# A transformer layer's first stage: from a simulated schedule to a written order of half-tile slots

## The chip, the cores and the metric

The kernel runs on one core of a Trainium2 chip. The metric is the device time of one execution in microseconds (us); the time of a kernel is the median of several runs. Engines are called PE (TensorE: products), PEld (its weight loads), DVE (VectorE), ACT (ScalarE), POOL (GpSimd) and SP (SyncE, which here issues DMAs). "Clock" is the share of the TensorE clock that was granted.

## What is computed

One layer of a diffusion transformer with two mixers side by side, for 2048 positions of width 1024, with 256 context positions that supply keys, values and a start state:

```python
mod = (silu(c) @ w_mod + b_mod)                    # sh1, sc1, g1, sh2, sc2, g2
h  = rmsnorm(x, norm1_g) * (1 + sc1) + sh1         # the same for ctx: hc
rq, rk, rv, rg, aq, ak, av = split(h @ w_in)       # hc gives rk, rv, ak, av only
ret = bidir_retention(rope(rq), rope(rk), rv)      # 4 heads of 128, chunks of 128
ret = groupnorm(ret) * gn_g * silu(rg)
att = attention(rope(rmsnorm(aq)), rope(rmsnorm(ak)), av)   # 8 heads of 64, 2 kv heads
x = x + g1 * (concat(ret, att) @ w_out)
x = x + g2 * (relu(h2 @ w_ff1) ** 2 @ w_ff2)       # h2: rmsnorm and modulate again
return rmsnorm(x, final_norm_g)
```

Everything is float32 in and out. Products that matter are made of float16 halves: an operand is split into a high and a low half, and three products (high by high, high by low, low by high) are added in PSUM.

## The kernel before, in words

The kernel has a first stage, an attention stage beside which retention and the output product run, and the feed-forward stage. The diff touches the first stage and a few lines of attention.

**First stage.** There are 18 tiles of 128 positions (2 of context, 16 of the sequence). First the modulation (class `Modulation`): 8.4 MB of `w_mod` come in 16 pairs of loads through four buffers of the tag `wst`, and small products with the activated `c` (L322) sum them into PSUM; `shift_and_scale` and `balance_h` make from them the factors `a1`, `s1` and the power of two `bk`. Then `h` is made per tile: load x, sum of squares (L405), root on POOL (L79, L80), scaling (L407), transposes (L432), modulation (L434, L435) and the split into halves (L70, L71). All 18 `h` tiles stay in SBUF.

Then the input product goes over six blocks of columns in the order `C_RV, C_RK, C_AKV, C_AQ, C_RG, C_RQ`; within a block it goes over the tiles (18 for RV, RK and AKV, 16 for the rest). A row, one tile by one block, is 24 products on PE (L504 to L506; AKV is half as wide). The weights of a block (class `Weights`) are loaded, their absolute sums are taken on ACT (L462), a scale is made from them and from `bk` (`scales`), and they are split on ACT and DVE (L488, L489). Behind a row, `post` evacuates PSUM on ACT and does what the column needs: rotary embedding on DVE and POOL (L535 to L542), norms, transposes on PE (L590, L621, L652), and stores to DRAM by SP.

Beside the rows, "extra" work is woven in by credits (`ROOM`, `share`): the later modulation rows (`later_rows`: load `wmr`, add on DVE at L356, product with ones at L368) and the largest absolute values of the other weights (`weight_maxima`: load `wm`, reduce on DVE at L711 or sum on ACT at L714). `value_parts`, `decay_tables` and `ff_scales` stand in the list `spare`, one step per row. `first_maximum` makes the row maxima of the first attention group in RG, 18 pieces, each a product into one PSUM bank and a reduce on DVE (L165, L178).

The program text of this stage does not fix the order on the engines: the framework orders its instructions by a simulated timeline (`schedule_with_timeline_sim=True`). DMAs are issued by SP; the tables for the rotary embedding, the biases and the gate stores are issued by ACT.

**Attention.** Its order is written out: `on(k, phase, fn)` puts a function into step k, and the steps are run in order under `tc.manual_schedule()`. There are 32 groups (a tile of queries and one of two key heads) of 18 steps each. Group n has its maxima ("piece" and "maximum") in steps 18n to 18n + 17, and its scores (L202, L203), exponentials (L208) and value products (L235, L236) from step 18n + 22 on. Group 0's maxima come from the first stage, so steps start near 18. Retention's forward states (L1098 to L1114) run beside groups 0 and 1.

Of the kernel before, what the change touches and what calls it, by code (L numbers as in the profile page):

```python
# [11 lines left out]
F32 = mybir.dt.float32  # L12
# [24 lines left out]
PSHIFT = 8  # L37

# [16 lines left out]
def layer_kernel(ctx: ExitStack, tc: tile.TileContext, a: dict, out: bass.AP):  # L55
# [85 lines left out]
    class Group:  # L141
# [15 lines left out]
        def minima(self, pool):  # L157
            self.nm = pool.tile([P, 2, 2, 5], F32, name="nm", tag="nm")
# [101 lines left out]
    with ExitStack() as st:  # L260
        xp = st.enter_context(tc.tile_pool(name="xp", bufs=4, reuse_waits="tile"))
        tp = st.enter_context(tc.tile_pool(name="tp", bufs=2, reuse_waits="tile"))
        hp = st.enter_context(tc.tile_pool(name="hp", bufs=1, reuse_waits="tile"))
        wp = st.enter_context(tc.tile_pool(name="wp", bufs=6, reuse_waits="tile"))
        sg = st.enter_context(tc.tile_pool(name="sg", bufs=3, reuse_waits="tile"))
# [9 lines left out]
        nc.sync.dma_start(cc, a["cc"])  # L275
        nc.scalar.activation(cc, cc, AF.Silu)
        cst = one.tile([P, KT, 2, 16], F32, name="cst")
        nc.vector.tensor_copy(cst, bc(cc.unsqueeze(3), [P, KT, 2, 16]))
        ones = one.tile([P, 32], F32, name="ones")
        nc.vector.memset(ones, 1.0)  # L280
        n1 = one.tile([P, KT], F32, name="n1")
        n2 = one.tile([P, KT], F32, name="n2")

# [8 lines left out]
        class Modulation:  # L292
# [4 lines left out]
            def __init__(self, q, b):  # L297
                self.q, self.w = q, {}
                self.b = b[:, q % 2 * self.W : (q % 2 + 1) * self.W]

            def load(self, k):
                if k == 0:
                    nc.gpsimd.memset(self.b[64:], 0.0)
                    for i in range(2):
                        c = i * D + self.q * self.W
                        src = a["b_mod"][0, c : c + self.W]
                        nc.scalar.dma_start(self.b[32 * i : 32 * i + 32], src.partition_broadcast(32))
                self.w[k] = sg.tile([P, 2, 2, self.W], F32, name="wst", tag="wst", bufs=4)
                for r in range(2):
                    rows = a["w_mod"][0, (k + r) * P : (k + r + 1) * P, : 2 * D]  # L310
                    src = rows.rearrange("p (i n) -> p i n", i=2)[:, :, self.q * self.W : (self.q + 1) * self.W]
                    nc.sync.dma_start(self.w[k][:, r], src)

            def product(self, k):
                if k == 0:
                    self.ps = psM.tile([P, 512], F32, name="mps", tag="mps")
# [7 lines left out]
            def end(self):  # L324
                nc.vector.tensor_tensor(self.b, self.ps[:, : self.W], self.b, op=ALU.add)

            def shift_and_scale(self):
                f = slice(2 * self.q, 2 * self.q + 2)
                scale = sm.tile([P, 2, 2], F32, name="sc", tag="sc")
                ps = columns(self.b, 2)  # L330
                for i, to in enumerate((s1[:, :, f].rearrange("p c j -> p j c"), scale)):
                    nc.vector.tensor_reduce(to, ps[:, :, i::2].rearrange("p j e c -> p j c e"), axis=AX.X, op=ALU.add)
# [4 lines left out]
        def later_rows(j, use):  # L337
# [4 lines left out]
            def load(i, k):  # L342
                w = x[i, k] = sg.tile([P, 2, 512], F32, name="wmr", tag="wmr", bufs=2)
# [3 lines left out]
            def add(i, k):  # L347
                w = x.pop((i, k))
                if k == 0:
                    x["acc"] = one.tile([P, 512], F32, name="macc", tag="mb")  # L350
# [6 lines left out]
                if (i, k) != (1, KT - 2):  # L357
                    load(*((i, k + 2) if k + 2 < KT else (1, 0)))

            def sums(i):  # L360
                if i == 0:
                    x["b"] = op.tile([P, 512], F32, name="mrow", tag="xs")
                    x["ps"] = psM.tile([P, 512], F32, name="mps", tag="mps")
                b, ps = x["b"], x["ps"]
                q = slice(32 * i, 32 * i + 32)
                src = a["b_mod"][0, (j + i) * 512 : (j + i + 1) * 512]
                nc.scalar.dma_start(b[q], src.partition_broadcast(32))
                mm(ps[q], ones, x["acc"], start=True, stop=True)  # L368
                if i == 1:
                    nc.vector.tensor_tensor(b[:64], ps[:64], b[:64], op=ALU.add)  # L370
                    use(b)

            steps = [lambda: load(0, 0)]
            for i in range(2):
                steps += [lambda i=i, k=k: add(i, k) for k in range(0, KT, 2)] + [lambda i=i: sums(i)]
            return steps

        def store_gate(r, b):
            for j in range(2):
                row = b[32 * j : 32 * j + 1, :]  # L380
                nc.scalar.dma_start(gate_d[r][j * 512 : (j + 1) * 512].unsqueeze(0), row)

        def shift2(b):
            ps = columns(b[:64], 4)
            nc.vector.tensor_copy(s2.rearrange("p (i j) -> p j i", i=2), ps[:, :, :, 0])

        def scale2(b):
            ps = columns(b[:64], 4)
            a, n = (x.rearrange("p (i j) -> p j i", i=2) for x in (a2, n2))
            nc.vector.scalar_tensor_tensor(a, ps[:, :, :, 0], 1.0, n, op0=ALU.add, op1=ALU.mult)  # L390

        def mod_steps():
            steps = later_rows(4, lambda b: store_gate(0, b)) + later_rows(6, shift2)
            return steps + later_rows(8, scale2) + later_rows(10, lambda b: store_gate(1, b))

        TILES = [("c", i) for i in range(NC)] + [("l", i) for i in range(NT)]

        def load_x(kind, i):

            x = xp.tile([P, D], F32, name=f"x_{kind}{i}", tag="x", bufs=4)  # L400
            src = a["ctx"] if kind == "c" else a["x"]
            nc.sync.dma_start(x, src[0, i * P : (i + 1) * P, :])
            ss = sm.tile([P, 1], F32, name="ss", tag="ss", bufs=2)
            junk = tp.tile([P, D], BF16, name="junk", tag="junk", bufs=1)
            nc.scalar.activation(junk, x, AF.Square, accum_out=ss)  # L405
            r = rsqrt(sm, ss, 1, 1.0 / D, "x")
            nc.vector.tensor_scalar_mul(x, x, r)  # L407
            return x

        bk = one.tile([P, KT], F32, name="bk")  # L410

        def balance_h():


            m = sm.tile([P, 2, KT], F32, name="hb", tag="hbm", bufs=1)
            for i, v in enumerate((a1, s1)):
                src = v.rearrange("p c k -> p k c")
                nc.vector.tensor_reduce(m[:, i], src, axis=AX.X, op=ALU.max, apply_absolute_value=True)
            nc.vector.scalar_tensor_tensor(bk, m[:, 0], 32.0, m[:, 1], op0=ALU.mult, op1=ALU.add)
            binade(bk)  # L420
            nc.vector.reciprocal(m[:, 0], bk)
            r = bc(m[:, 0].unsqueeze(1), [P, 2, KT])
            for v in (a1, s1):
                nc.vector.scalar_tensor_tensor(v, v, 4096.0, r, op0=ALU.mult, op1=ALU.mult)

        def part_h(kind, x, h, k, n):

            c = 1 if kind == "c" else 0
            f = slice(k, k + n)
            ps = psT.tile([P, 4, P], F32, name="psx", tag="psx")[:, :n]  # L430
            for j in range(n):
                nc.tensor.transpose(ps[:, j], x[:, (k + j) * P : (k + j + 1) * P], ident)  # L432
            t = tp.tile([P, 4, P], F32, name="t", tag="t")[:, :n]
# [1389 lines left out]
```

## Time and profile before

| | |
|---|---|
| median of 3 runs | 2941.21 us (2940.58 to 2946.13) |
| the profiled execution: its time | 2945.99 us |
| its span, first to last instruction | 2944.2 us |
| mean granted clock | 0.98 |
| first and last input product (pso) of the first stage | start at 65.7 and 663.5 us |
| first scores of attention | 674.1 us |

The span is some 1.8 us shorter than the device time of the same execution. In rows of busy time by stretch the columns are the stretch, its length, the busy us of PE, PEld, DVE, ACT and POOL with the number of instructions, the granted clock, the mean busy share of the 16 DMA engines, and the GB/s that they moved. In rows of groups, what follows the bar is the busy time and the mean duration in ns, then the idle time of the engine just before, with what ended it.

### The profile page before, as it was taken

The numbers are of one execution on the slowest core, as the hardware profiler recorded it, in microseconds if no ns is written. First come the engines' busy times: TensorE is split into PE (matmuls) and PEld (weight loads), VectorE is DVE, ScalarE is ACT, GpSimd is POOL, SyncE is SP. The second block draws the span as 40 slices with busy tenths as digits, with TensorE's granted clock in tenths as the row PEclk, the third lists the DMA queues.
The fourth block names the chain that finished last, engine by engine and source line by source line (L and its number), as shares of the span: only waits on it lengthen the run. The fifth ranks groups of instructions, "written<-read, shape, count | busy, mean of one in ns | idle before, by whom it ended". The sixth has DMA issues, their size and how long they took to land. (4 is left out here: it accounts for less than half of the span.)

```text
span 2944.2 us, 45374 instructions
## 1 busy us (share of the span) xinstructions
PE 2749.6 (93%) x17152; PEld 1460.0 (50%) x17152; DVE 2097.5 (71%) x3305; ACT 1429.7 (49%) x2418; POOL 1524.6 (52%) x1288
## 2 busy tenths in 40 slices
PE   5999998897799999999999899999999899999998
PEld 1544743345566665556666444444444344444443
DVE  4635665658987777777776477778777777777776
ACT  2552463135777777777777333333332333333332
POOL 1423672225865677886566556664443444444332
PEclk6999999999999999999999999999999999999999
DMA  9476457536412123332211723331114511111111
GB/s 298 141 228 208 149 162 225 164 89 211 126 48 67 56 64 113 95 103 81 87 50 51 273 91 101 104 104 63 49 51 154 174 59 47 56 49 51 58 43 58
DMA packets 252250, 323.89 MB, mean 110 GB/s; under 512 B 105463, under 2 KB 161015, under 8 KB 250238
## 3 DMA queue, kind: packets, MB, share of 16 engines
q1 hardware_dynamic: 241750, 313.49, 33.0%
q10 hardware_dynamic: 10280, 7.48, 0.9%
q8 instruction: 135, 2.21, 0.3%
q14 instruction: 85, 0.70, 0.1%
HBM read 249.45 MB, written 71.46 MB: 109 GB/s over the span
## 5 line engine op out<-in xcount | busy, mean ns | idle before, releaser
L178 DVE TENSOR_REDUCE nm<-mp 128x1 f32<-128x512 f32 (+1 forms) x576 | 390.7, 684 | 155.9 <-PE mp L165 127.5
L219 POOL TENSOR_TENSOR plo<-p,phi 128x1024 f16<-128x1024 f32 x160 | 353.3, 2209 | 172.6 <-ACT phi L212 134.5
L208 ACT ACTIVATE p<-st 128x512 f32<-128x512 f32 x576 | 338.5, 597 | 190.8 <-PE st L203 119.4
L1597 PE MATMUL pd<-w2hi,uhi 128*128 128x512 f16 x1024 | 388.0, 379 | 13.7 <-DVE acc L1600 13.6
L1598 PE MATMUL pd<-w2lo,uhi 128*128 128x512 f16 x1024 | 388.0, 379 | 0.6 <-DVE w2lo L71 0.6
L1599 PE MATMUL pd<-w2hi,ulo 128*128 128x512 f16 x1024 | 388.1, 379 | 0.0
L1600 DVE SCALAR_TENSOR_TENSOR acc<-pd,sc,acc 128x512 f32<-128x512 f32 x512 | 366.3, 738 | 5.6 <-PE pd L1599 5.6
L1537 PE MATMUL pu<-hf,w1f 128*128 128x512 f16 x896 | 340.8, 380 | 2.5 <-DVE q L1560 2.0
L1538 PE MATMUL pu<-hf,w1f 128*128 128x512 f16 x896 | 340.9, 380 | 0.0
L1539 PE MATMUL pu<-hf,w1f 128*128 128x512 f16 x896 | 340.7, 380 | 0.0
L212 ACT ACTIVATE phi<-p 128x1024 f16<-128x1024 f32 x288 | 303.9, 1055 | 0.0
L506 PE MATMUL pso<-whi,h 128*128 128x512 f16 (+1 forms) x816 | 298.1, 366 | 4.0 <-DVE h L71 3.9
L504 PE MATMUL pso<-whi,h 128*128 128x512 f16 (+1 forms) x816 | 297.3, 365 | 2.2 <-ACT h L70 2.2
L505 PE MATMUL pso<-wlo,h 128*128 128x512 f16 (+1 forms) x816 | 298.3, 366 | 0.2 <-DVE wlo L489 0.2
L235 PE MATMUL o<-wv,plo 128*128 128x65 f16 x2304 | 236.1, 194 | 23.9 <-POOL plo L219 16.7
L221 DVE TENSOR_TENSOR plo<-p,phi 128x512 f16<-128x512 f32 x256 | 240.7, 941 | 18.5 <-ACT phi L212 15.9
L236 PE MATMUL o<-wv,phi 128*128 128x129 f16 x2304 | 243.9, 221 | 0.0
L235 PEld LDWEIGHTS <-plo 128*128 128x128 f16 x2304 | 206.8, 98 | 58.7 <-POOL plo L219 25.9
L202 PE MATMUL st<-qr,ks 128*128 128x512 f16 x576 | 219.5, 381 | 15.0 <-ACT p L208 14.9
L165 PE MATMUL mp<-ks,qr 128*128 128x512 f16 x512 | 196.8, 384 | 38.3 <-DVE nm L178 38.2
L203 PE MATMUL st<-qr,ks 128*128 128x512 f16 x576 | 219.9, 382 | 0.1
L1549 POOL TENSOR_TENSOR r<-r 128x512 f32<-128x512 f32 x64 | 66.4, 1041 | 295.6 <-ACT r L1548 295.6
(338 smaller groups left out, 5407.2 us busy)
## 6 DMA issues: line engine op xcount, KB each, us to landing
wm<-in_w_ff SPq DMA_DIRECT2D x64, 512.0 KB, 5.1
w1r<-in_w_ff SPq DMA_DIRECT2D x64, 512.0 KB, 4.2
ws<-in_w_ff SPq DMA_DIRECT2D x124, 256.0 KB, 3.3
wmr<-in_w_mod SPq DMA_DIRECT2D x32, 512.0 KB, 4.9
hf<-hp SPq DMA_DIRECT2D x56, 256.0 KB, 3.1
hf<-hf SPq DMA_DIRECT2D x14, 1024.0 KB, 6.3
wst<-in_w_in SPq DMA_DIRECT2D x20, 512.0 KB, 5.4
orv<-rv SPq DMA_DIRECT2D x35, 256.0 KB, 3.3
```

The source lines that it names most:

```text
L178: nc.vector.tensor_reduce(dst, src, axis=AX.X, op=ALU.max, negate=True)
L208: nc.scalar.activation(self.p[kt // 2][:, kt % 2], self.s.pop(kt), AF.Exp, scale=HD**-0.5)
L212: nc.scalar.activation(hi, self.p[j], AF.Copy)
L219: nc.gpsimd.tensor_tensor(lo, p, hi, op=ALU.subtract)
L235: mm(o[:, : HD + 1], lo[:, i, c], v[:, : HD + 1], start=False, stop=False)
L1537: mm(pu[i], whi, hi, start=k == 0, stop=False)
L1538: mm(pu[i], whi, lo, start=False, stop=False)
L1539: mm(pu[i], wlo, hi, start=False, stop=k == 3)
L1597: mm(ps, uh, wh, start=f == 0, stop=False)
L1598: mm(ps, uh, wl, start=False, stop=False)
L1599: mm(ps, ul, wh, start=False, stop=f == NF - 1)
L1600: nc.vector.scalar_tensor_tensor(acc[:, c], ps, sc2, acc[:, c], op0=ALU.mult, op1=ALU.add)
```

## The change

The first stage gets a written order. Every row is two half-tile slots q (2s and 2s + 1 for row s); `at(q, step, fn)` puts a function into a slot, and the steps of a slot are run in the order "dma", "mm", "turn", "copy", "work", "mix", "extra", "store" under `tc.manual_schedule()`. In detail:

- A class `Row` replaces `post`, `rope` and `head_norm`: each part of what follows a row has a slot of its own, up to nine after the row's last product.
- `Modulation.load` puts the weights into the buffers of `h` (tags h2 to h17), which are not in use yet: all 16 pairs of loads are issued at once, with x tiles 0 to 3 and the first block of `w_in` between them. The biases come whole. `balance_h` becomes part of `shift_and_scale`, per quarter.
- In the start, the sums of the first `w_in` block and the first halves of three `h` tiles are made beside the modulation; the second halves and the splits follow it.
- Later rows and maxima have fixed slots: in RK and RG one later-rows load and one reduce of maxima per tile; the |w| sums on ACT four before RK, then one a tile in AKV and AQ, two in RG. `value_parts` is in AQ, `decay_tables` and `ff_scales` in RQ.
- `first_maxima` makes the maxima of three attention groups (`EARLY = 3`): group 0 in RG, groups 1 and 2 in RQ, in two PSUM banks; attention leaves out these pieces, so steps 18 to 53 have none. Groups 1 and 2 load their queries again in attention.
- PSUM: `psM` has two banks of the tag `mp` and one `mps` (one before); `psO` has 3 banks instead of 5. `tp` has 4 buffers instead of 2, `sg` 2 instead of 3 by default.
- All DMAs of the stage are issued by SP. The sum of the identity in `tables` is on POOL instead of DVE.

The diff, cut to its core:

```diff
+EARLY = 3
...
-        psM = st.enter_context(tc.tile_pool(name="psM", bufs=1, space=PSUM, reuse_waits="tile"))
+        psM = st.enter_context(tc.tile_pool(name="psM", bufs=2, space=PSUM, reuse_waits="tile"))
...
-        psO = st.enter_context(tc.tile_pool(name="psO", bufs=5, space=PSUM, reuse_waits="tile"))
+        psO = st.enter_context(tc.tile_pool(name="psO", bufs=3, space=PSUM, reuse_waits="tile"))
+        st.enter_context(tc.manual_schedule())
+        slots, base = [], {}
+        for n, col in enumerate(ORDER):
+            base[col] = 2 * len(slots)
+            slots += [(n, m) for m, t in enumerate(TILES) if t[0] == "l" or col not in (C_RQ, C_RG, C_AQ)]
+        base["end"] = 2 * len(slots)
+        STEPS = ("dma", "mm", "turn", "copy", "work", "mix", "extra", "store")
+        plan = {}
+        def at(q, step, fn, *args):
+            plan.setdefault((q, step), []).append((fn, args))
...
             def load(self, k):
-                self.w[k] = sg.tile([P, 2, 2, self.W], F32, name="wst", tag="wst", bufs=4)
+                n = 2 + self.q * 4 + k // 2
+                self.w[k] = hp.tile([P, 2, 2, self.W], F32, name=f"wm{n}", tag=f"h{n}")
...
         def later_rows(j, use, qs):
+            for n, q in enumerate(qs):
+                i, k = n // 4, n % 4 * 2
+                at(q - 3, "dma", load, i, k)
+                at(q, "extra", add, i, k)
+                if k == KT - 2:
+                    at(q + 1, "turn", sums, i)
...
+        for m in range(3, len(TILES)):
+            q = 2 * (m - 3)
+            if m > 3:
+                at(max(0, q - 6), "dma", load_x, m)
+                at(max(0, q - 3), "copy", squares, m)
+                at(max(0, q - 2), "work", root, m)
+                at(max(1, q - 1), "mix", normal, m)
+            for p in range(2):
+                at(q + p, "turn", turn_h, m, p)
+                at(q + p + 1, "work", modulate, m, p)
+                at(q + p + 2, "copy", high_h, m, p)
+                at(q + p + 2, "copy", low_h, m, p)
...
+            def prepare(self, q0, q1):
+                for i in range(4):
+                    at(q0 + 2 + i, "dma", self.fetch, 2 * i)
+                    at(q0 + 9 + 2 * i, "extra", self.bound, 2 * i)
+                at(q0 + 17, "work", self.greatest)
+                at(q0 + 19, "turn", self.spread)
+                at(q0 + 20, "work", self.scales)
+                for k, q in zip(range(0, KT, 2), (q0 + 22, q0 + 24, q1 - 2, q1 - 1)):
+                    at(q, "mix", self.split, k)
...
+        class Row:
+            def __init__(self, s):
+                q = 2 * s + 2
+                for half in range(2):
+                    at(2 * s + half, "mm", self.products, half)
+                at(q, "copy", self.evacuate)
+                if self.col in (C_RK, C_RQ):
+                    at(q - 3, "dma", self.table, a["ret_cs"], P)
+                    at(q, "work", self.rope, H, P)
+                    at(q + 1, "work", self.rope_add)
+                    if self.col == C_RK:
+                        at(q + 2, "store", self.store, rk_d)
+                    at(q + 2, "turn", self.turn)
+                    at(q + 3, "copy", self.turned)
+                    at(q + 4, "store", self.store_turned, qt_d if self.col == C_RQ else kt_d)
...
         def maxima(i, q):
+            at(q - 4, "store", load)
+            at(q, "extra", greatest)
...
+        def first_maxima(n, pool, tag, bufs, q_load, qs):
+            g = groups[n]
+            at(q_load, "dma", g.load, pool, tag, bufs)
+            at(q_load, "dma", g.minima, kp)
+            for i, q in enumerate(qs):
+                at(q, "turn", g.piece, i, psM, "mp")
+                at(q + 1, "work", g.maximum, i)
...
+        row_slots = [rk + 2 * i + 1 for i in range(18)] + [rg + 2 * i + 1 for i in range(14)]
+        big = [rk + 2 * i for i in range(18)] + [rg + 2 * i for i in range(14)]
+        sums = [rk - 8 + 2 * i for i in range(4)] + [akv + 2 * i for i in range(18)]
+        sums += [aq + 2 * i + 1 for i in range(16)] + [rg + 28, rg + 30]
+        first_maxima(0, xp, "x", 4, rg + 8, [rg + 13 + i for i in range(18)])
+        first_maxima(1, sg, "wst", 4, rq, [rq + 4 + i * 12 // 17 for i in range(18)])
+        first_maxima(2, sg, "wst", 4, rq + 10, [rq + 17 + i * 12 // 17 for i in range(18)])
...
+        modulation(0)
+        mods[0].end()
+        modulation(1, (ready, 0), (ready, 1))
...
+        modulation(3, (halves_h, 0, (2,)), (first.bound, 2), (first.bound, 4), (first.bound, 6))
+        turn_h(0, 1)
+        mods[3].end()
+        mods[3].shift_and_scale()
+        first.greatest()
+        first.spread()
+        modulate(0, 1)
+        first.scales()
+        high_h(0, 1)
+        low_h(0, 1)
+        first.split(0)
+        first.split(2)
+        halves_h(1, (1,))
+        first.split(4)
+        first.split(6)
+        halves_h(1, (2,))
+        ready(3)
         balance(g2)
...
+        for q in range(min(plan)[0], base["end"] + 8):
+            for step in STEPS:
+                for fn, args in plan.pop((q, step), ()):
+                    fn(*args)
...
         for n, g in enumerate(groups):
             k = NK * n
             if n > 0:
-                on(k - 14, "dma", g.load)
+                on(k - 14 if n >= EARLY else k + NK - 6, "dma", g.load)
+            else:
+                on(k + NK, "begin", g.load)
+            if n >= EARLY:
                 on(k - 1, "late", g.minima, sm)
```

More of the change, by code (lines that the diff above doesn't have):

```diff
@@ L392, in mod_steps @@
[L392 to L400, printed above, removed]
+                    x["ps"] = psM.tile([P, 512], F32, name="mps", tag="mps", bufs=1)
+                mm(x["ps"][32 * i : 32 * i + 32], ones, x["acc"], start=True, stop=True)
@@ L426, in part_h @@
[L426 to L433, printed above, removed]
-            nc.vector.tensor_tensor(t, ps, bc(a1[:, c, f].unsqueeze(2), [P, n, P]), op=ALU.mult)
-            nc.gpsimd.tensor_tensor(t, t, bc(s1[:, c, f].unsqueeze(2), [P, n, P]), op=ALU.add)
-            split16(h[:, 0, f], h[:, 1, f], t)
@@ L659, in value_parts @@
+        for s in range(len(slots)):
+            Row(s)
+        def value_parts(q0):
             x = {}
@@ new lines, in layer_kernel @@
+        nc.sync.dma_start(cc, a["cc"])
+        nc.sync.dma_start(n1, a["n1"])
+        rows = sg.tile([P, D], F32, name="rows", tag="wm")
+        nc.gpsimd.memset(rows[64:], 0.0)
+        for i in range(2):
+            nc.sync.dma_start(rows[32 * i : 32 * i + 32], a["b_mod"][0, i * D : (i + 1) * D].partition_broadcast(32))
+        nc.scalar.activation(cc, cc, AF.Silu)
+        nc.vector.tensor_copy(cst, bc(cc.unsqueeze(3), [P, KT, 2, 16]))
+        nc.vector.memset(ones, 1.0)
+        first = weights[0]
```

688 lines of the change are left out of this document (344 added, 344 removed).

## The prediction, made before the changed kernel ran

> **What bounds the kernel now.** I read the page first, then busy time by stretches over the first stage, then single instructions in order of time, then groups by line and shape, then the waits of two stretches.
>
> ```profile
> span 2944.2 us, 45374 instructions
> PE 2749.6 (93%) x17152; PEld 1460.0 (50%) x17152; DVE 2097.5 (71%) x3305; ACT 1429.7 (49%) x2418; POOL 1524.6 (52%) x1288
> ```
>
> TensorE is the bound on average; what the first stage is worth must be read from its own stretches. Here are its six column blocks, RV, RK, AKV, AQ, RG, RQ (columns: stretch, its length, busy us of each engine, granted clock, DMA share, GB/s):
>
> ```profile
> 75.00:182.80 107.80, 106.13 (x552) 55.40 (x550) 70.07 (x106) 62.42 (x121) 45.27 (x57) 1.00 0.52 170
> 182.80:294.40 111.60, 106.68 (x514) 49.95 (x513) 47.41 (x76) 37.43 (x70) 31.04 (x30) 1.00 0.66 214
> 294.40:351.70 57.30, 54.17 (x477) 46.24 (x475) 39.95 (x121) 28.36 (x78) 36.65 (x83) 1.00 0.49 150
> 351.70:443.90 92.20, 91.21 (x453) 45.02 (x451) 61.07 (x99) 54.65 (x103) 72.33 (x79) 1.00 0.51 156
> 443.90:559.00 115.10, 94.44 (x401) 40.43 (x400) 67.53 (x85) 30.69 (x59) 24.01 (x20) 0.93 0.71 222
> 559.00:664.00 105.00, 94.70 (x451) 45.67 (x450) 60.67 (x160) 28.95 (x54) 30.14 (x34) 0.97 0.30 91
> ```
>
> TensorE's own rate, in order of time (start, duration, engine, line):
>
> ```profile
> 659.64 0.60 PE L590 MATMUL psx<-ident,ys 128*128 128x128 f32 x4
> 660.08 0.38 PE L505 MATMUL pso<-wlo,h 128*128 128x512 f16 x1
> 660.29 0.38 PE L506 MATMUL pso<-whi,h 128*128 128x512 f16 x1
> 660.51 0.38 PE L504 MATMUL pso<-whi,h 128*128 128x512 f16 x1
> ```
>
> The next 512-wide product starts 0.215 us after the one before; four transposes take 0.44, so 0.11 each. A row of 24 products is 5.16. AQ needs 16 x 5.16 + 64 x 0.11 = 89.6 of its 92.2: TensorE fills it. RG needs 82.6 and takes 115.1, RQ 89.6 and takes 105.0. The slack is there, and in the start:
>
> ```profile
> 0.00:10.00 10.00, 3.27 (x16) 0.78 (x16) 0.47 (x3) 1.50 (x2) 1.29 (x9) 1.00 0.69 198
> 10.00:20.00 10.00, 7.71 (x44) 2.03 (x42) 2.59 (x13) 0.00 (x0) 1.18 (x3) 1.00 1.00 322
> 20.00:30.00 10.00, 5.82 (x38) 1.48 (x34) 0.83 (x4) 1.15 (x2) 0.70 (x3) 0.81 0.98 320
> 30.00:40.00 10.00, 5.74 (x28) 1.41 (x26) 3.00 (x7) 3.44 (x6) 2.59 (x7) 0.50 1.05 364
> 60.00:70.00 10.00, 4.19 (x15) 2.42 (x14) 9.90 (x16) 8.24 (x14) 4.34 (x5) 0.50 0.89 315
> ```
>
> ```profile
> 45.49 1.82 PE L322 MATMUL mps<-wst,cst 128*32 128x256 f32 x8 [3.62 <-DMA wst<-in_w_mod]
> 47.64 0.63 ACT L462 ACTIVATE junk<-wst 128x512 bf16<-128x512 f32 x1 [8.52 <-DMA wst<-in_w_in]
> 60.15 5.01 ACT L488 ACTIVATE whi<-wst,ws 128x512 f16<-128x512 f32 x8 [6.51 <-DVE ws L480]
> 64.74 2.73 DVE L489 SCALAR_TENSOR_TENSOR wlo<-wst,ws,whi 128x512 f16<-128x512 f32 x4
> 65.73 0.61 PE L504 MATMUL pso<-whi,h 128*128 128x512 f16 x1 [1.85 <-ACT h L70]
> 70.11 0.61 PE L506 MATMUL pso<-whi,h 128*128 128x512 f16 x1 [3.35 <-DVE h L71]
> ```
>
> The modulation ends at 47.3, and only then come the sums of |w_in|, the scales, and the split: 18 us without a product.
>
> **Part 1, the start.** Ahead of the last modulation weights the queue now carries 8.39 MB of w_mod, three x tiles (1.57), w_in's first block (2.10) and about 0.3 of biases: 12.4 MB. The loads for later rows and maxima that ran between them are gone. At the rates above 12.0 MB are in by 40 us, so the last load lands near 41 and its products end at T = 43, 4 us earlier. All loads without waits don't make them faster: the share was already 1.0. The sums of |w_in| now lie before T. From T to the first split half I take 8 us: ACT's row at 60.15 shows the scales' chain as 6.5 us of idle, with four sums of later rows of 0.75 in it that are gone, so 3.5; the last sum, its transposes and the balance ahead of it are about as long; and one modulate (0.7) now stands within. Then ACT's eight halves (5.0) run beside VectorE's eight (0.68 each, 5.5) and the second halves of three h tiles (3.6), so VectorE ends near T + 17. The order puts the transposes of tile 3 between the two halves of row 0, and they wait for that tile's scaling, 0.8 more. With 0.44 and 12 products row 0 ends at T + 20.8 = 63.8. Then 17 rows and 15 tiles of 8 transposes, 87.7 + 12.8: RV ends at 164.3 where it ended at 182.8. Between T + 8 (51) and T + 24 for row 0's end I take this chain, since the 60-to-70 row shows VectorE full (9.90) in the same work.
>
> **Part 2, the blocks.** Every step now has a half-tile slot. The durations:
>
> ```profile
> L711 DVE TENSOR_REDUCE wmx<-wm 128x1 f32<-128x1024 f32 x32 | 39.0, 1219 | 47.2 <-DMA wm<-in_w_ff 47.2
> L356 DVE SCALAR_TENSOR_TENSOR macc<-wmr,cc,macc 128x512 f32<-128x512 f32 x56 | 46.9, 838 | 13.7 <-DMA wmr<-in_w_mod 13.0
> L178 DVE TENSOR_REDUCE nm<-mp 128x1 f32<-128x512 f32 x16 | 10.9, 683 | 3.7 <-PE mp L165 3.7
> L368 PE MATMUL mps<-macc,ones 128*32 128x512 f32 x16 | 10.1, 719 | 6.5 <-DVE macc L356 6.5
> L714 ACT ACTIVATE junk<-wm 128x1024 bf16<-128x1024 f32 x40 | 42.2, 1056 | 67.7 <-DMA wm<-in_w_out 24.2 <-DVE hs_q L549 23.7 <-DMA wm<-in_w_ff 18.4
> L632 ACT ACTIVATE xs<-pso,wm 128x256 f32<-128x256 f32 x18 | 8.4, 465 | 9.2 <-DMA av<-xs 3.2 <-POOL rv_k L79 3.1 <-PE pso L506 2.0
> wm<-in_w_ff SPq DMA_DIRECT2D x64, 512.0 KB, 5.1
> wmr<-in_w_mod SPq DMA_DIRECT2D x32, 512.0 KB, 4.9
> ```
>
> RK: 18 x 5.16 + 7.0 + half of L368's 10.1 = 104.9 on TensorE. Each row now also carries one load of maxima and one of later rows, 512 KB each, with two stores of 256 and a table of 128: 1.76 MB with the next weights. The RK row moved 214 GB/s at share 0.66, or 324 at full share, so DMA needs 5.4 us a row beside 5.8. VectorE: 2 x 0.838 + 1.219 + rope, under 5. I take 107; ends 104.9 and 118 (DMA at 270 GB/s).
> AKV: half the width, so an estimate of 46.7 + 36 x 0.11 = 50.7 on TensorE. Most of the forty |w| sums move here and to AQ: 1.06 on ACT and a short read, beside 0.465 and two smaller, some 2.3 a row, with the next weights' sums and halves about 3.0, little over TensorE's 2.8: 54 (50.7 to 60).
> AQ: 89.6; POOL, 72.3 of 92.2 busy, has the same work and covers it. I take 91 (89.6 to 95).
> RG: 82.6 + 18 maxima (3.9) + 5.0 = 91.5. VectorE's second half is the fullest: 1.68 + 1.22 + two maxima 1.37 + gate bound, of the maxima's form, 0.68 = 4.9 a row of 5.7. With two banks TensorE no longer waits for each maximum. I take 93.5 (91.5 to 110).
> RQ: 89.6 + 36 maxima of the next two groups (7.7) = 97.3; VectorE gets 36 x 0.683 = 24.6 more on the 60.7 there; 85 fits in 99 (97.3 to 108).
> Sum: 164.3 + 107 + 54 + 91 + 93.5 + 99 = 608.8 against 664.0: 55.2 less.
>
> Edits at nothing, with SP's issue:
>
> ```profile
> 61.67 0.37 SPq L345 DMA_DIRECT2D wmr<-in_w_mod  x1
> ```
>
> 76 small DMAs pass from ACT's queue to SP's. At about 0.4 us an issue SP has some 2.2 us a row, covered by 5.8; without that cover each costs its 0.4. A store that waits on SP holds the loads behind it, and VectorE's sums wait for those; they are issued three or four slots (8.7 us and more) before use, against landings of 5.1. Four table sums move to POOL, idle three quarters of RQ. Three buffers instead of five for products are freed by ACT in the next slot.
>
> **Part 3, attention's first groups.** The 36 maxima leave the first two groups of scores:
>
> ```profile
> 664.00:674.00 10.00, 4.06 (x16) 2.25 (x14) 6.14 (x10) 4.55 (x7) 4.30 (x5) 0.70 0.74 236
> 674.00:705.60 31.60, 27.45 (x222) 18.91 (x222) 28.71 (x55) 20.74 (x32) 19.35 (x12) 0.93 0.51 165
> 705.60:743.50 37.90, 29.65 (x280) 22.48 (x280) 32.25 (x68) 21.44 (x34) 26.65 (x20) 0.95 0.78 262
> 743.50:773.60 30.10, 25.67 (x265) 19.30 (x264) 28.81 (x48) 22.80 (x37) 24.35 (x16) 1.00 0.47 146
> ```
>
> VectorE bounds both (28.7 of 31.6, 32.3 of 37.9) and loses 12.3 in each. Next are ACT in the first (20.7) and DMA in the second (0.78 x 37.9 = 29.6) with POOL (26.7). I take 27 and 32, and 2 off the gap before: 12 in all, between 3 and 20.
>
> **Sum.** 55.2 + 12 = 67 off the profiled execution's 2945.99: 2879. The median of the runs is 4.8 lower, so 2874.
>
> **Rivals.**
> 1. Slower: VectorE, in order, stands at the head of its queue for a load in RK and RG, and TensorE behind it.
>
> ```profile
> DVE wmx L711 <- DMA wm<-in_w_ff: 45.0, 25, 6.3
> PE mp L165 <- DVE nm L178: 13.1, 6, 3.7
> PE mps L368 <- DVE macc L356: 5.8, 1, 5.8
> ```
>
> In RG it waited 45.0 in 25 waits, 1.8 each. If all 64 loads (32 of each kind, two buffers each) cost that, and all of it reached TensorE, it is 115: 2989. From 67 / 64 = 1.05 us each, that is landings of 9.8 us instead of 5.1, the gain is gone. Against it: the loads were issued as buffers came free, 25 in a single block; now one of a kind comes each row.
> 2. RK, RG and RQ stay at 111.6, 115.1 and 105.0: 4.6 + 21.6 + 6 = 32 back, 2906. The granted clock speaks for it: it fell to 0.93 in RG, among waits of up to 5.8. [...]
> 3. The weights landing at once brings nothing, and RV ends at 182.8 as before, since DMA was full: 2892.
> 4. TensorE's bare sums hold in all blocks (10 less), attention gives 20 (8 less), row 0 ends 8 earlier: 2848.
>
> **How the numbers follow.** Forecast (2855 to 2895) 0.60, rival 4 0.10, rival 3 0.09, rival 2 0.10, slower 0.08, and 0.03 for mishaps that just eat the gain. The range, 2846 to 2912, takes in all but the last two and a little of rival 2. A change under 0.2% (6 us) can't be told from none here. Faster 0.88, same 0.03, slower 0.09.
>
> **What would show it.** First pso product near 51, the last of row 0 near 64; last pso near 609 where it was 664; RK with a DMA share of 0.9 or more and clock 1.00; DVE's waits for wm and wmr well under 47 and 13; no PE wait on nm in RG; scores of the first two groups in 27 and 32. Wrong if DVE waits for wm or wmr in RK and PE's clock falls there, or if SP stands on a store while loads are due.

## The result, and the profile after

The changed kernel takes 2898.15 us in the median of four runs (2894.32 to 2899.49); beside it on the same chip the kernel before took 2942.22 (2940.58 to 2946.13). The ratio is 0.9846, with a 95% interval of 0.9829 to 0.9863: 44 us faster. One execution of the kernel before and one of a variant below, at clocks near 0.6, took over 4300 us and stand in no median or ratio here. The two profiled executions are 51.7 apart, 2945.99 and 2894.32; the stages below are compared on these two.

The page of the kernel after (span, then busy time of each engine) shows the same work in less time:

```profile
span 2892.2 us, 45242 instructions
PE 2728.7 (94%) x17152; PEld 1459.3 (50%) x17152; DVE 2094.2 (72%) x3324; ACT 1428.9 (49%) x2418; POOL 1528.8 (53%) x1289
```

The first stage's blocks, again RV, RK, AKV, AQ, RG, RQ, in the columns used before:

```profile
72.00:171.80 99.80, 97.05 (x501) 50.82 (x500) 52.33 (x84) 53.17 (x98) 44.74 (x52) 1.00 0.44 144
171.80:275.70 103.90, 103.90 (x499) 49.44 (x498) 73.11 (x103) 27.80 (x57) 29.26 (x30) 1.00 0.88 289
275.70:335.60 59.90, 55.02 (x483) 47.03 (x482) 33.10 (x109) 46.63 (x112) 34.39 (x80) 1.00 0.79 243
335.60:427.40 91.80, 89.31 (x447) 44.73 (x445) 71.47 (x120) 57.76 (x109) 74.95 (x82) 1.00 0.60 186
427.40:523.40 96.00, 92.81 (x426) 40.95 (x425) 75.56 (x108) 25.42 (x48) 27.13 (x23) 1.00 0.75 237
523.40:624.00 100.60, 98.23 (x486) 48.38 (x484) 66.07 (x156) 27.21 (x50) 30.28 (x35) 1.00 0.26 81
```

Read these against the rows of before: RK went from 111.6 to 103.9 and TensorE is busy in every microsecond of it, while DMA moved 289 GB/s where it moved 214. RG went from 115.1 to 96.0, RQ from 105.0 to 100.6 with 36 maxima more in it. AKV is the one block that became longer, 57.3 to 59.9, and its ACT column rose from 28.4 to 46.6. The granted clock is 1.00 in all six. (The stretches end up to 0.5 us before the evacuation of a block's last row; from evacuation to evacuation RQ takes 100.3 and RV, from row 0 on, 104.6.)

The start, by stretches and then in order of time:

```profile
10.00:20.00 10.00, 7.44 (x44) 1.93 (x42) 3.36 (x14) 2.30 (x4) 1.60 (x4) 0.83 1.07 371
20.00:30.00 10.00, 7.30 (x48) 2.47 (x46) 3.39 (x14) 1.15 (x2) 1.27 (x3) 0.83 1.08 364
30.00:40.00 10.00, 5.28 (x40) 2.39 (x38) 4.53 (x16) 2.59 (x6) 2.60 (x3) 0.83 1.08 363
```

```profile
38.09 2.81 PE L334 MATMUL mpm<-wm,cst 128*32 128x256 f32 x24
48.75 0.58 PE L638 MATMUL pso<-whi,h 128*128 128x512 f16 x1 [0.42 <-ACT whi L535]
51.74 0.38 PE L640 MATMUL pso<-whi,h 128*128 128x512 f16 x1
59.78 0.69 DVE L473 TENSOR_TENSOR h<-t,h 128x512 f16<-128x512 f32 x1 [1.88 <-ACT h L469]
61.73 0.75 DVE L450 TENSOR_SCALAR x_l<-x_l,ry_x 128x1024 f32<-128x1024 f32 x1 [1.26 <-POOL ry_x L81]
62.63 1.09 PE L459 MATMUL psx<-ident,x_l 128*128 128x128 f32 x4 [10.51 <-DVE x_l L450]
63.51 0.63 PE L638 MATMUL pso<-whi,h 128*128 128x512 f16 x1
63.94 0.63 PE L639 MATMUL pso<-wlo,h 128*128 128x512 f16 x1
```

The last modulation product ends at 40.9 (47.3 before). The first input product starts at 48.75 (65.7 before). The second half of row 0 then stands behind transposes of tile 3 that wait 10.5 us for that tile's scaling: row 0 is evacuated at 67.7, and the gain of 17 us in the first product is one of 11 us when RV ends (182.8 to 171.8).

The groups of the added work, by line and shape, and the longest waits for VectorE of TensorE in RG:

```profile
L381 DVE SCALAR_TENSOR_TENSOR macc<-wmr,cc,macc 128x512 f32<-128x512 f32 x56 | 43.7, 781 | 3.4 <-DMA wmr<-in_w_mod 2.3
L815 DVE TENSOR_REDUCE wmx<-wm 128x1 f32<-128x1024 f32 x32 | 38.7, 1209 | 2.3 <-DMA wm<-in_w_ff 2.3
L818 ACT ACTIVATE junk<-wm 128x1024 bf16<-128x1024 f32 x40 | 41.9, 1047 | 7.6 <-DMA wm<-in_w_ff 7.4
L818 ACT ACTIVATION_READ_ACCUMULATOR junk<-wm 128x1 f32 x40 | 7.5, 187 | 0.0
```

```profile
PE mps L386 <- DVE macc L381: 1.7, 2, 0.9
PE psx L691 <- DVE ys L723: 1.5, 2, 1.2
```

VectorE's waits for `wm` fell from 47.2 to 2.3 and for `wmr` from 13.0 to 2.3, at landings of 5.2 and 5.5 us that are no shorter than before (5.1 and 4.9). TensorE waits for no maximum in RG any more, where it had waited 13.1.

Attention: the gap before its first scores, then its first two groups of scores, and the waits of the second group:

```profile
624.00:632.00 8.00, 1.61 (x10) 1.26 (x9) 5.30 (x11) 3.96 (x6) 5.67 (x8) 0.84 0.69 223
632.00:658.10 26.10, 23.79 (x204) 18.14 (x203) 16.86 (x37) 20.74 (x33) 16.37 (x11) 0.85 0.61 191
658.10:693.90 35.80, 28.18 (x265) 21.95 (x264) 19.81 (x53) 20.71 (x32) 27.50 (x21) 0.90 0.92 296
```

```profile
DVE sf L1245 <- DMA sf<-sf: 12.9, 6, 4.5
PEld bank L1235 <- POOL okw L1229: 7.8, 5, 3.7
POOL okw L1229 <- DMA ork<-rk: 5.0, 4, 2.1
```

VectorE lost 11.9 and 12.4 us in the first two groups, as the moved maxima say; the groups became 5.5 and 2.1 us shorter (31.6 and 37.9 before). In the second one VectorE now stands 12.9 us for stores of the retention state (4.0 before), and TensorE's weight loads 7.8 for POOL's weighting of retention keys (2.4 before).

So of 51.7 us, 40.2 are there at the start of the last input product (663.5 before, 623.3 now), 48.7 when the fourth group begins (773.7, 725.0), and the last 3 lie in stages that the diff doesn't touch; runs of one kernel differ by as much.

### The profile page after: what moved, and what is told of

The parts are those of the page before. It is cut to its first block, busy times and chain, and to the rows that moved or that the text cites. A ratio compares the mean times of both kernels' runs of the same rounds, so it can differ in the third digit from the quotient of the medians.

```text
span 2892.2 us, 45242 instructions
## 1 busy us (share of the span) xinstructions
PE 2728.7 (94%) x17152; PEld 1459.3 (50%) x17152; DVE 2094.2 (72%) x3324; ACT 1428.9 (49%) x2418; POOL 1528.8 (53%) x1289
## 5 line engine op out<-in xcount | busy, mean ns | idle before, releaser
L638 PE MATMUL pso<-whi,h 128*128 128x512 f16 (+1 forms) x816 | 294.9, 361 | 0.4 <-ACT whi L535 0.4
L640 PE MATMUL pso<-whi,h 128*128 128x512 f16 (+1 forms) x816 | 294.5, 361 | 0.0
L237 PEld LDWEIGHTS <-plo 128*128 128x128 f16 x2304 | 206.7, 98 | 57.3 <-POOL plo L221 25.6
L238 PEld LDWEIGHTS <-phi 128*128 128x128 f16 x2304 | 205.8, 98 | 20.0 <-issue 0.3
```

The lines of the kernel that those rows point to most:

```text
L237: mm(o[:, : HD + 1], lo[:, i, c], v[:, : HD + 1], start=False, stop=False)
L238: mm(o, hi[:, i, c], v[:, :VW], start=False, stop=last)
```

## The experiments

Ratios are to the kernel before on the same chip, with the 95% interval; 0.9846 is the change itself, and a second set of its runs gave 0.9834 [0.9821, 0.9848], with 2894.15 us. Block times are from each kernel's profile, by the stretches shown or by evacuations, which differ by up to 0.5 us.

**Is it the written order at all?** The same program text, ordered by the simulated timeline:

```diff
-        st.enter_context(tc.manual_schedule())
```

> The changed program of the first stage, with its slots as program order, but handed back to the simulated timeline for ordering. If the written order makes the gain of the first stage (my theory), the last input product starts near 655 us instead of 624, and the time is 2925 to 2945. If what the stage does makes it (loads at once, one stream of each kind per row, two banks), whatever the order (rival), the last product stays within 10 us of 624 and the time within 10 of 2898.

Measured: 2939.83 us, 0.9988 [0.9977, 0.9999]. Nearly all of the gain is gone. RK, AQ and RQ of this kernel, and its waits of TensorE over RK to RQ:

```profile
166.80:289.90 123.10, 108.08 (x501) 50.28 (x499) 62.76 (x90) 35.91 (x71) 29.08 (x30) 0.94 0.72 233
357.30:469.50 112.20, 92.06 (x435) 43.80 (x434) 83.45 (x128) 50.33 (x97) 66.67 (x78) 0.92 0.55 174
572.30:668.70 96.40, 96.40 (x479) 47.79 (x478) 53.59 (x116) 19.36 (x31) 30.04 (x31) 1.00 0.21 68
```

```profile
PE psx L690 <- DVE inv L781: 12.8, 1, 12.8
PE psx L690 <- DVE ys L685: 8.2, 2, 6.5
PE pso L638 <- DVE wlo L535: 6.6, 1, 6.6
```

The same work, buffers, banks and loads: RK takes 123.1 instead of 103.9, AKV 67.4 instead of 59.9, AQ 112.2 instead of 91.8, RG 102.8 instead of 96.0; RQ is 4.2 shorter and RV ends 5.0 earlier (166.8). The sum, 19.2 + 7.5 + 20.4 + 6.8 - 4.2 - 5.0 = 44.7, is the difference of the ends of RQ (668.7 and 624.0). The order is what keeps TensorE from standing 6 to 13 us behind one late step on VectorE. Not the start, though: here too the last modulation product ends at 41 and row 0 near 68. So the order on the engines isn't what moved the modulation forward; what of the rest did wasn't tried, but for the buffers, which come next.

**Do the loads gain by being issued at once?** The weights go back to four buffers in turn:

```diff
-                self.w[k] = hp.tile([P, 2, 2, self.W], F32, name=f"wm{n}", tag=f"h{n}")
+                self.w[k] = hp.tile([P, 2, 2, self.W], F32, name=f"wm{n}", tag=f"h{2 + (n - 2) % 4}")
```

> The changed kernel with the modulation weights in four of h's buffers in turn instead of sixteen, so that loads wait for products. Theory: DMA is at its rate either way (363 to 371 GB/s from 10 to 40 us; 320 to 364 before, with four buffers), so the last modulation product moves by 1 to 4 us and the time by no more than 4. Rival: loads that wait leave gaps, and the last product comes 8 us or more later.

Measured: 2897.58 us, 0.9849 [0.9836, 0.9863], not to be told from the change. Two stretches of its start (the one between them moved 365 GB/s):

```profile
10.00:20.00 10.00, 7.04 (x42) 1.86 (x42) 3.37 (x14) 2.30 (x4) 1.65 (x4) 0.83 1.08 375
30.00:40.00 10.00, 5.29 (x33) 2.02 (x31) 4.34 (x16) 1.72 (x5) 1.74 (x2) 0.66 1.07 360
```

With a fourth of the buffers the queue moves the same 360 to 375 GB/s; the first product is at 49.1 and row 0 at 68.2. The buffers of `h` bring nothing here.

**Does the second bank for maxima suffice?** The kernel before, with two banks for them (and four instead of five for products):

```diff
-        psM = ... bufs=1 ...    psO = ... bufs=5 ...
+        psM = ... bufs=2 ...    psO = ... bufs=4 ...
```

> The kernel before with two PSUM banks instead of one for the first group's maxima (four instead of five for the input products). If the single bank made RG long (115 us before, 96 now), RG falls to about 100 and the time to about 2927. If RG was long for the order around it (VectorE waited 45 us for maxima loads there), RG stays at 110 or more and the time within 5 us of 2942.

Measured: 2945.74 us, 1.0013 [1.0001, 1.0025]. Its RG:

```profile
446.00:554.60 108.60, 91.34 (x401) 39.59 (x400) 66.65 (x83) 30.62 (x59) 23.34 (x20) 0.95 0.73 225
```

RG falls less far than to the 100 expected of the bank. The bank shortens it by 6.5 (115.1 to 108.6), and RQ, from 105.0 to 111.4, gives it back: the last product stands at 665.5. In RG VectorE still waits for the loads of maxima:

```profile
DVE wmx L711 <- DMA wm<-in_w_ff: 37.8, 24, 4.9
```

By itself the second bank brings nothing in the total. What it is worth in the written order, a run of the change with one bank would show; there is none.

**Are the moved maxima worth it?** Only group 0's maxima stay in the first stage:

```diff
-EARLY = 3
+EARLY = 1
...
-        first_maxima(1, sg, "wst", 4, rq, ...)
-        first_maxima(2, sg, "wst", 4, rq + 10, ...)
```

> The changed kernel with EARLY = 1: maxima of groups 1 and 2 stay in attention, as before. RQ falls from 100.6 to about 92 (36 products of 0.215 and their waits). If moving the maxima pays as forecast, attention's first two groups and the gap ahead of them go back from 70 to 79 and the time is 0 to 4 us above 2898 (gain and price nearly equal). If the gain of 8.7 seen there comes from elsewhere, the groups stay near 70 and the time falls by 8.

Measured: 2891.38 us, 0.9819 [0.9805, 0.9834], 3 to 7 us less than the two sets of the change (their intervals overlap this one a little), where 0 to 4 more was expected. RQ, the gap and the first two groups:

```profile
522.30:611.70 89.40, 89.40 (x445) 44.40 (x443) 45.31 (x121) 27.20 (x50) 30.29 (x35) 1.00 0.27 87
611.40:623.30 11.90, 4.84 (x19) 2.56 (x18) 7.91 (x15) 4.56 (x7) 5.67 (x8) 0.66 0.68 216
623.30:654.20 30.90, 27.70 (x224) 19.40 (x223) 26.96 (x55) 20.80 (x32) 19.80 (x12) 0.91 0.51 164
654.20:691.50 37.30, 29.95 (x280) 22.57 (x278) 32.23 (x68) 21.36 (x34) 26.55 (x20) 0.95 0.78 265
```

RQ without them is 89.4, TensorE's own 89.6 of the prediction, so 36 maxima cost it 11.0 (100.3 and 89.3 from evacuation to evacuation), where the pieces alone are 7.7. Gap and groups take 80.1 instead of 70.7: they won 9.4. The moved maxima lose 1.6 there, and 4.6 by the last group's scores (1548.5 and 1553.1).

**One group instead of two:**

```diff
-EARLY = 3
+EARLY = 2
...
-        first_maxima(2, sg, "wst", 4, rq + 10, ...)
```

> The changed kernel with EARLY = 2: only group 2's maxima go back, into the steps of group 1's scores. Theory: those steps are now bound by DMA (share 0.92), not by VectorE (19.8 of 35.8 busy), so the 12.3 us of reduces fit in: group 1 stays within 2 us of 35.8, RQ falls by 4 to 5, and the time is 2 to 5 us below 2898. Rival: VectorE or TensorE bounds them, group 1 grows by 5 or more and nothing is gained or it is slower.

Measured: 2894.69 us, 0.9833 [0.9815, 0.9851], the change's own ratio. No profile shows its blocks; the combination below has EARLY = 2 as well, and there the second group grows by 4.1 instead of staying within 2.

**What holds AKV?** Nine of its eighteen |w| sums go to RV and RQ:

```diff
-        sums = [rk - 8 + 2 * i for i in range(4)] + [akv + 2 * i for i in range(18)]
-        sums += [aq + 2 * i + 1 for i in range(16)] + [rg + 28, rg + 30]
+        sums = [rk - 24 + 2 * i for i in range(12)] + [akv + 4 * i for i in range(9)]
+        sums += [aq + 2 * i + 1 for i in range(16)] + [rg + 28, rg + 30, rq + 2]
```

> The changed kernel with nine of the |w| sums in AKV, one per two rows, instead of eighteen; eight more go to RV and one to RQ. Theory: AKV is 60 us instead of 51 to 54 since ACT waits there for the loads of these sums (7.2 us in 8 waits, landings of 5.2 us in two buffers at 2.8 us a row) and the keys' halves stand behind: AKV falls to 53 to 55, RV grows by at most 2, the time falls by 4 to 6. Rival: AKV's long chain over ACT, VectorE and POOL bounds it without the loads: AKV stays at 58 or more.

Measured: 2889.36 us, 0.9824 [0.9811, 0.9838]. In the change, these were AKV's waits:

```profile
DVE kn L736 <- ACT kh L735: 19.4, 14, 4.1
ACT junk L818 <- DMA wm<-in_w_ff: 7.2, 8, 2.6
PE psx L741 <- DVE kn L736: 4.5, 5, 1.4
```

and here its row:

```profile
276.90:329.90 53.00, 52.81 (x478) 46.75 (x477) 32.25 (x107) 37.31 (x94) 35.24 (x80) 1.00 0.61 180
```

AKV falls from 59.9 to 53.0, with TensorE full; RV ends 1.2 later and AQ is 1.0 longer, and the last group of scores is 5.0 earlier. The chain was ACT (a sum, waiting for its load) ahead of ACT's `kh`, ahead of VectorE's `kn`, ahead of TensorE's transposes. VectorE still waits 15.7 us for `kh` here, but TensorE only 0.2 for `kn`. The edit takes away the sums' own time and their loads together, so how much each was worth isn't shown.

**What holds row 0?** Tile 3 is made ready between the splits, and the splits come before the halves of tiles 1 and 2:

```diff
         first.greatest()
+        squares(3)
         first.spread()
         modulate(0, 1)
         first.scales()
+        root(3)
...
         first.split(0)
+        normal(3)
         first.split(2)
-        halves_h(1, (1,))
         first.split(4)
         first.split(6)
-        halves_h(1, (2,))
-        ready(3)
+        halves_h(1, (1, 2))
```

> The changed kernel with the start reordered: tile 3's squares, root and scaling come before the splits instead of after the second halves of h tiles 1 and 2, and all four splits before those halves. Theory: the 10.5 us in which TensorE stands at tile 3's transposes is a chain that only the order makes; row 0 ends near 57 instead of 67.6, and 7 to 11 us stay in the time: 2888 to 2891. Rival: the splits and halves bound the start anyway (VectorE's work to 60 us), row 0 ends no earlier than 63 and rows 1 and 2 give back the rest: 0 to 3 us.

Measured: 2894.38 us, 0.9841 [0.9828, 0.9855]; row 0 is evacuated at 65.4 instead of 67.7. Two rows of transposes in time:

```profile
55.29 0.66 PE L459 MATMUL psx<-ident,x_l 128*128 128x128 f32 x4 [1.73 <-DVE t L464]
64.13 0.63 PE L459 MATMUL psx<-ident,x_l 128*128 128x128 f32 x4 [2.49 <-DVE x_l L450]
```

The wait of 10.5 is gone and waits for other work of VectorE stand in its place. It gains 2.3 us of the 4 that the prediction was short there, as the rival said; the total can't tell it from the change.

**The three together** (one group moved less, nine sums moved, the start):

> The three edits of start, |w| sums and EARLY = 2 together. If each reason holds, they add: 9 + 5 + 3, and the time is near 2881 (2876 to 2888). If they hit the same limit, less than 10 in all.

Measured: 2883.82 us, 0.9804 [0.9791, 0.9817]. RQ, then groups 0 and 1:

```profile
515.80:609.60 93.80, 93.23 (x463) 46.17 (x462) 55.07 (x138) 28.22 (x52) 30.31 (x35) 1.00 0.26 82
617.60:647.40 29.80, 24.57 (x208) 18.16 (x206) 20.57 (x40) 21.02 (x33) 19.25 (x12) 0.90 0.60 192
647.40:687.30 39.90, 30.73 (x280) 23.18 (x280) 32.26 (x68) 21.58 (x34) 27.57 (x20) 0.93 0.76 253
```

That is in the expected range. On the same chip the sums alone are 8.2 us below the four-buffer kernel, the start alone 3.2 and the three together 13.8, so they add up within the noise. AKV is 52.3 and RQ 93.8, so the first of the two moved groups costs RQ 4.4 us and the second 6.8 (89.4, 93.8, 100.6 with none, one, two). The second group of scores, which makes its maxima itself again, takes 39.9: 4.1 more. The first takes 29.8, 3.7 more: group 2's maxima begin in its last steps.

**No group moved, nine sums moved, and a finer start** (`squares(3)` and `root(3)` as in the start above, the second halves of tiles 1 and 2 laid between the splits, `balance(g2)` in slot 20):

```diff
         modulate(0, 1)
+        turn_h(1, 1)
         first.scales()
...
         first.split(0)
+        modulate(1, 1)
+        normal(3)
+        turn_h(2, 1)
         first.split(2)
-        halves_h(1, (1,))
+        modulate(2, 1)
+        high_h(1, 1)
         first.split(4)
+        low_h(1, 1)
         first.split(6)
-        halves_h(1, (2,))
-        ready(3)
-        balance(g2)
+        high_h(2, 1)
+        low_h(2, 1)
+        at(20, "extra", balance, g2)
```

> The changed kernel with EARLY = 1, the |w| sums of AKV spread, and the start's chain interleaved (tile 3's scaling early; the modulates of tiles 1 and 2 between the splits; the balance of the norm weights moved to slot 20). Theory: the start still lost time since VectorE stood twice for POOL and ACT in the second halves of tiles 1 and 2; row 0 ends near 59 instead of 65.4 with the first reordering; last product near 596; time 2874 to 2880. Rival: TensorE's banks for transposes hold row 0 to 63 or later, and the time is 2881 to 2886.

Measured: 2884.22 us, 0.9796 [0.9782, 0.981], 58 us below the kernel before and 10 below the change on the same chip (2894.15). A stretch of its start:

```profile
50.00:60.00 10.00, 8.95 (x36) 3.99 (x35) 10.00 (x14) 6.46 (x11) 5.12 (x5) 0.75 0.17 63
```

Row 0 is evacuated at 61.5 where 59 was expected, and the last product starts at 602.2 where it was 596; the time lies in the rival's range, though row 0 comes before the rival's 63. From 50 to 60 VectorE is busy throughout: the limit of this stretch. This and the three together can't be told apart.

**What holds attention's second group?** Three ideas were DMA's rate (share 0.92), POOL, and the buffers of the retention state. First, the output weights, whose loads and gating lie there, come 12 steps earlier:

```diff
-    output_weights(44)
+    output_weights(32)
```

> The changed kernel with the output weights' loads and gating (5.2 MB) begun 12 steps earlier, out of the steps of group 1's scores into those of group 0. Theory: group 1 is bound by DMA (share 0.92 in 35.8 us), so it falls to 30 to 32 and group 0 grows from 26.1 to at most 28: 2 to 5 us less in all. Rival: the retention's chain over POOL, TensorE and VectorE with its stores bounds it, at 34 or more whatever else is loaded.

Measured: 2902.0 us, 0.9859 [0.9845, 0.9874]. Groups 0 and 1 take 33.4 and 33.8, together 67.2 where the change on that chip took 25.6 and 37.2, together 62.8. The second group:

```profile
665.20:699.00 33.80, 26.61 (x265) 20.93 (x263) 23.58 (x55) 21.35 (x34) 29.42 (x21) 0.95 0.84 258
```

It became 3.4 shorter, less than the theory said, and the first group 7.8 longer: together 4.4 lost. So the output weights do cost the group in which they lie, and the edit doesn't tell their loads from their gating. Then their gating passes from POOL to VectorE, which has room:

```diff
-            nc.gpsimd.tensor_tensor(w_[k, n], w_[k, n], g, op=ALU.mult)
+            nc.vector.tensor_tensor(w_[k, n], w_[k, n], g, op=ALU.mult)
```

> The changed kernel with the gating of the output weights (16 products of 128x512, 1.27 us each on POOL) on VectorE, which has room in the steps of group 1's scores (19.8 of 35.8 us busy). If POOL (27.5 of 35.8 busy, its waits reach TensorE by okw) bounds these steps, group 1 falls to 33 or less and the time by 2 to 4. If the loads and stores there bound them (POOL itself waits for ork, VectorE 12.9 us for stores of sf), group 1 stays within 1 us of 35.8 and the time within 2.

Measured: 2900.54 us, 0.9851 [0.9834, 0.9869]. Groups 0 to 2 take 25.7, 39.4 and 33.8; the second is longer and neither expectation came. Its row and three of its waits:

```profile
658.30:697.70 39.40, 29.18 (x264) 22.61 (x264) 25.84 (x56) 21.81 (x34) 26.12 (x18) 0.87 0.84 271
```

```profile
DVE sf L1245 <- DMA sf<-sf: 10.0, 3, 3.8
PEld bank L1235 <- POOL okw L1229: 8.6, 5, 3.5
POOL okw L1229 <- DMA ork<-rk: 6.4, 5, 2.3
```

POOL is busy 26.1 of 39.4 us instead of 27.5 of 35.8, and TensorE waits for its `okw` as long as ever: `okw` itself waits for `ork` from DRAM. So POOL's total is not the bound, and DMA's rate is neither shown nor ruled out. More buffers for `sf`, which waits for its stores, and for `ork`, so that its loads start earlier, weren't tried: what bounds the second group stays open.

The changed kernel was run once more beside two of these, for their comparison:

> The changed kernel once more, beside the two others on the same chip: 2898, within 3 us.

Measured: 2894.15 us (2891.94 to 2894.83), with the same blocks: the last product at 622.9, group starts at 631.7, 657.3 and 694.5. Two sets of runs of this one kernel on two chips lie 4 us apart.

## Why the prediction was right, and where its terms were off

The forecast was 2874 with 2855 to 2895 as its own range; 2898.15 lies 3 us outside that and inside the whole range, 8 below the second rival's 2906. The mechanism held: an order in which each load and each step on VectorE has its slot keeps TensorE full, shown by taking the order away (2939.83). The size was too large by 24 us. Of these, 9 lie in no term: the sum starts from an execution 4.8 above its kernel's median, and the profiled execution of the change lies 3.8 below its own. Between the profiled executions 15.3 of the 67 didn't come, and in the first stage 15.2 of the 55.2. The terms of that sum can be set beside the measured ones; one error, RK's, went the other way and hid 3 us of the rest:

| term | predicted | measured | off by |
|---|---|---|---|
| row 0's end | 63.8 | 67.7 | +3.9 |
| from there to RV's end | 100.5 | 104.1 | +3.6 |
| RK | 107 | 103.9 | -3.1 |
| AKV | 54 | 59.9 | +5.9 |
| AQ | 91 | 91.8 | +0.8 |
| RG | 93.5 | 96.0 | +2.5 |
| RQ | 99 | 100.6 | +1.6 |

(The measured column is by the stretches shown; RQ's end is 0.7 behind the last product's start.)

- **The start.** T was 40.9 where 43 was forecast and the first product 48.75 where it was 51: both 2 us earlier. The chain from there to row 0's end failed: 20.8 us from T were forecast and it took 26.8. The prediction did have the second half of row 0 behind VectorE's whole list and tile 3's scaling, so most of the 10.5 us wait is in its sum (by its numbers TensorE stands some 7 us there). Three sizes were off. VectorE's list ended at T + 19.6 instead of T + 17, since it stood twice 1.88 us for ACT's halves of `h`, which a sum of busy times leaves out. The scaling let the transposes start 2.2 later instead of 0.8, with 1.26 of waiting for POOL's root. The transposes and 12 products took 5.1 instead of 3.0: behind the wait the products start 0.43 us apart (63.51 and 63.94), twice the 0.215 that the prediction counted. Even with the list laid finer, row 0's evacuation is at 61.5, with VectorE full.
- **RK** was put above TensorE's own 104.9 for fear of DMA; TensorE, busy throughout, took 103.9. DMA moved 289 GB/s at share 0.88, near the 0.9 that was named, and VectorE's waits for `wm` and `wmr` came to 2.3 each over the whole kernel.
- **AKV** is the largest miss. The term counted a sum at 1.06 us with "a short read", and that read is 0.187 each, so 1.23; but the sum of busy times was not the point: ACT was busy 46.6 of 59.9. A sum standing in front of `kh` delays a chain over three engines, and the loads of these sums were sometimes late (7.2). Moving nine of them gave 53.0. In part this is the mechanism of the first rival, an engine standing in order before a load, on ACT and in AKV instead of on VectorE in RK and RG; the part of the sums' own time isn't known.
- **RG and RQ.** TensorE has no wait for a maximum in RG, as forecast. The two banks alone were worth 6.5 of RG's 19.1 and nothing in the total. RQ's maxima were priced by TensorE's pieces, 7.7, with 1.7 more for VectorE: they cost 11.0.
- **Attention.** 12 forecast, 9.4 came up to the third group's scores, 0.9 of which that group gave back (31.0 where it took 30.1). From the last input product's start the gap is 8.8 instead of 10.6, 1.8 for the 2 forecast; the other terms are the first group, 5.5 for 4.6, and the second, 2.1 for 5.9. The prediction named DMA at share 0.78 and POOL as next in line and set 32; the waits for single transfers that came are 12.9 us (stores of `sf`) and 5.0 (loads of `ork`), and what bounds the group is open.
- **Edits at nothing.** SP's 76 further DMAs, the four sums on POOL and three product buffers instead of five show no wait of TensorE in RK at all and none over 1.2 us for VectorE in RG. They were not tried one by one, so that they cost nothing is read from the trace only. SP did stand on stores, the sign of being wrong that the prediction named: 34.2 us in 11 waits for ACT's `xs` between 72 and 624. It cost TensorE little, whose waits of all kinds come to 15.5 there, the longest 1.7 and none for an evacuation. In AKV SP stood 14.4 us in 12 waits for a buffer of a rotary table; with nine sums moved it stood 19.9, and AKV was 53.0, so this isn't what made AKV long.

Of the rivals, the third was right about the buffers (the four-buffer kernel is the same) and wrong about RV's end, since the modulation ended 6.4 us earlier all the same. Why it did is open in part. From 10 to 40 us the rows give 10.98 MB where they gave 10.06 before; 0.92 MB at 364 GB/s is 2.5 us. The rest, some 4, is not a shorter list: 2.1 MB of loads for later rows and maxima are gone from ahead of the last weights, and 2.1 MB of `w_in` stand there in their place. SP had issued the last weights by 34.6 us instead of 38.8. The fourth rival, TensorE's bare sums in all blocks, came in RK alone. The second did not come: RK, RG and RQ all became shorter, and the clock is 1.00 in each. Of the clock, to which it pointed, the traces show this: from RK to RQ the longest wait of TensorE in the change is 1.7 us, at 1.00 in every block, while the simulated order has single waits of 6.5, 6.6 and 12.8, with the clock at 0.94, 0.95, 0.92 and 0.97 in RK, AKV, AQ and RG, and 1.00 in RQ, where TensorE is busy throughout (96.40 of 96.40). Whether a wait lowers the clock, and what that would cost beside the wait itself, no run shows.

## What to carry to other kernels

With several engines in one chain, TensorE's stalls came here less from an engine's sum of work than from one late item in front of a short, urgent one; fix the order, give every load a slot a few slots ahead of its use, and look in each block for the wait on TensorE and follow it back over two or three engines. Moving work off a busy stage pays only what its next limit leaves: price it at both ends, the stage that takes it (11.0) and the one that loses it (9.4), before doing it. When a price is put together from busy times, add the waits inside the chain: row 0's came 6 us later after T than its sum said. A better order is worth trying with the parts taken out again: here leaving two groups' maxima where they were is 3 to 7 us faster than the change, and with the sums and the start laid anew as well it is 10.

## What the runs showed that was not expected

- The load queue moves more in the start: 363 to 371 GB/s at a share of 1.07 to 1.08 in the change, and the same with four buffers or the simulated order (375 and 364), against 322 and 320 at 1.00 and 0.98 from 10 to 30 us before. So a share of 1.0 was not yet the full rate, as the prediction took it to be. What slowed it before was not tried.
- A sum by ACT over 128x1024 takes 1.047 us and the read of its accumulator 0.187 more, 18% on top.
- A wait on VectorE moves rather than vanishes: with the wait of 10.5 us for tile 3 taken away, row 0 gained 2.3, and with the list laid finer, 6.2.
